# A depthwise filter's shared sum moved to ScalarE and GpSimd, and a float32 preparation made in three passes

## The chip, the cores and the metric

The kernel runs on one core of a Trainium2 chip. The metric is device time of one execution in microseconds (us), the median over the runs. The engines of the core that matter here are TensorE (PE in the profile, with PEld for its weight loads), VectorE (DVE), ScalarE (ACT), GpSimd (POOL) and SyncE (SP, which issues the transfers). SBUF is the on-chip memory, PSUM the accumulators that TensorE writes.

## What is computed

A two-layer decoder trunk on 1024 tokens of width 1024. Only the first layer's mixer (the convolution layer) and the weights of the attention into 256 memory tokens are touched; the other parts (forgetting attention, squared-ReLU MLPs, final norm) follow and are the same in both kernels.

```python
def conformer_conv(h, w_pw1, b_pw1, w_dw, b_dw, ln_g, ln_b, w_pw2, b_pw2):
    u = h @ w_pw1 + b_pw1
    a, gate = jnp.split(u, 2, axis=-1)
    u = a * jax.nn.sigmoid(gate)
    u = lax.conv_general_dilated(
        u, w_dw[:, None, :].astype(u.dtype),
        window_strides=(1,), padding=[(CONV_WIDTH - 1, 0)],
        dimension_numbers=("NWC", "WIO", "NWC"),
        feature_group_count=D_MODEL) + b_dw
    u = jax.nn.silu(layernorm(u, ln_g, ln_b))
    return u @ w_pw2 + b_pw2
...
def memory_cross_attention(h, mem_n, w_q, w_k, w_v, w_o):
    q = (h @ w_q).reshape(B, S, MEM_HEADS, MEM_HEAD_DIM)
    k = (mem_n @ w_k).reshape(B, MEM_LEN, MEM_HEADS, MEM_HEAD_DIM)
    v = (mem_n @ w_v).reshape(B, MEM_LEN, MEM_HEADS, MEM_HEAD_DIM)
    s = jnp.einsum("bshd,bmhd->bhsm", q, k).astype(jnp.float32) / math.sqrt(MEM_HEAD_DIM)
    p = jax.nn.softmax(s, axis=-1)
    o = jnp.einsum("bhsm,bmhd->bshd", p.astype(v.dtype), v).reshape(B, S, D_MODEL)
    return o @ w_o
```

The convolution has 31 taps on each of 1024 channels.

## The kernel before

**Layout.** Features lie on the 128 partitions, so a 1024x1024 array is 8 chunks of 128 features by 1024 tokens, handled in two halves of 512 tokens. The residual stream `X` is a grid of 128x512 tiles.

**Split products.** Most products run in three passes of a reduced float32 type (`F32R`): each operand is split into a high part (a cast by ScalarE) and a low part (source minus high part, by VectorE, in `low`, line 148), and `passes` and `product` (up to line 269) issue low by high, high by low and high by high into one PSUM accumulator. `product` takes a plain float32 operand as a tuple of one and then issues one matmul.

**The convolution layer** (`conv_layer`). For each chunk `m` of 8: `gated_unit` makes the first product (48 matmuls for each of the gate and the value half), ScalarE takes the sigmoid (line 368), VectorE multiplies (line 370) and writes `u` with even and odd tokens apart, two buffers of it. `weights` fetches the next chunk's weights and splits them (`wh` on ScalarE, `wl` on VectorE, two of each per chunk). Then `convolve` computes the 31 taps for the even and the odd output tokens with a shared sum: `d0` and `d1` are the differences of even and odd input tokens (lines 393 and 394), `both` is the sum over 16 pair weights times the odd tokens (one multiplication on line 396, 15 multiply-adds on line 400), and each half of the output is `both` plus 16 or 15 multiply-adds with the differences (line 408). All of this is on VectorE. The 31 multiply-adds go into two accumulators, the output tiles `X[:, m, 0]` and `X[:, m, 1]`, so two independent chains stand side by side. Line 354 adds the finished chunk to the layer norm's token sums. After the eighth chunk comes the layer norm of both halves (lines 310 to 318 and `sum_of_squares`, with the split for the next product), and then the second product `pw2` (384 matmuls of 512 columns, added to the residual on line 324).

**The memory preparation** (`memory_matrices`, a generator; for the two layers and four heads each). It folds the query weights with the keys and the value weights with the output weights, 64 weight pieces of 128x1024 (`praw`, 512 KB each) in all: four for keys and values (line 461 forward: 32 matmuls of 256 columns per head), two for `mqk` (16 matmuls of 256 columns) and two for `mvo` (8 matmuls of 512 columns). Results leave through ScalarE (`o`, lines 483 and 501) and transfers to DRAM. Everything is plain float32: nothing of it is split. `conv_layer` advances the generator by `next(prep)`: four of its 32 steps stand ahead of the first convolution, two in each chunk, and the twelve left stand between the layer norm and `pw2`.

**What sets the order.** The instructions are traced in the order of the program; a planner then fixes each engine's order ahead of time. It goes by that order as a priority and by its own estimate of when an instruction can start, so that an instruction further down is put in where an engine would otherwise stand still. `tc.high_priority` moves a few small ones ahead. On the chip, each engine then runs its list in order. PSUM's eight banks are shared out as four to the preparation, two to the products of the convolution layer, two to small work (`ps`).

Of the kernel before, what the change touches and what calls it, by code (L numbers as in the profile page):

```python
# [12 lines left out]
F32 = mybir.dt.float32  # L13
F32R = mybir.dt.float32r
# [72 lines left out]
def trunk(ctx, tc, a, out):  # L87
# [16 lines left out]
    def col(name, i):  # L104
        return par[:, COLS[name] + i : COLS[name] + i + 1]
# [38 lines left out]
    def banks(n):  # L144
        return tc.tile_pool(name="pm", bufs=n, space=PSUM, reuse_waits="tile")
# [39 lines left out]

    def add_squares(acc, ch):

        sq = nrm.tile([P, HALF], F32, name="sq", tag="t", bufs=4)
# [101 lines left out]
        dve.tensor_tensor(X[:, m, sl], t, X[:, m, sl], op=ALU.add)  # L290


    def conv_layer(pm, prep):
        with tc.tile_pool(name="conv", bufs=2) as cp:
            for sl in HALVES:
                next(prep)
                load_x(X, a["xT"], sl)
            def padded():

                u = cp.tile([P, 2, (PAD + S) // 2], F32, name="u")  # L300
                pool.memset(u[:, :, : PAD // 2], 0.0)
                return u

            pairs = tap_sums(cp)

            def layer_norm(s, acc):

                nm = nrm.tile([P, 4], F32, name="nm")
                with tc.high_priority(offset=SMALL_FIRST):
                    dve.tensor_scalar(nm, token_mean(acc), -1.0, None, op0=ALU.mult)  # L310
                nmb = spread(nm)
                C = [X[:, m, HALVES[s]] for m in range(NCH)]
                for c in C:
                    dve.tensor_tensor(c, c, nmb, op=ALU.add)
                rb = spread(inverse_rms(C, LN_EPS))
                for m, c in enumerate(C):
                    dve.tensor_tensor(c, c, rb, op=ALU.mult)
                    act.activation(c, c, AF.Silu, bias=col("ln_b", m), scale=col("ln_g", m))
                    split(*(y.rearrange("p (n s) -> p s n", s=2)[:, s, :] for y in ss[m]), c)

            def add_x(m, sl, t):
                x = nrm.tile([P, HALF], F32, name="x", tag="t", bufs=4)
                nc.sync.dma_start(x, a["xT"][:, m, sl])
                dve.scalar_tensor_tensor(
                    X[:, m, sl], t, col("pw2_b", m), x, op0=ALU.add, op1=ALU.add
                )
# [12 lines left out]
            for m in range(NCH):  # L339
                if m:  # L340
                    u = padded()
                    for sl in HALVES:
                        gated_unit(pm, cp, m, ahead, hs, u[:, :, PAD // 2 :], sl)
                if m + 1 < NCH:
                    ahead = gate_weights(m + 1)
                for _ in range(2):
                    next(prep, None)

                convolve(cp, m, u, pairs[:, m])
                for s, sl in enumerate(HALVES):  # L350
                    if m == 0:
                        act.copy(acc[s], X[:, m, sl])
                    else:
                        dve.tensor_tensor(acc[s], acc[s], X[:, m, sl], op=ALU.add)
# [28 lines left out]
        dve.tensor_tensor(sums[:, :, :n], two[:, :, :, 0], two[:, :, :, 1], op=ALU.add)  # L383
        return sums

    def convolve(cp, m, u, sums):


        n, k = S // 2, TAPS // 2
        even, odd = u[:, 0, :], u[:, 1, :]  # L390
        d0 = cp.tile([P, n + k], F32, name="d0")
        d1 = cp.tile([P, n + k - 1], F32, name="d1")
        dve.tensor_tensor(d0, even[:, : n + k], odd[:, : n + k], op=ALU.subtract)
        dve.tensor_tensor(d1, even[:, 1 : n + k], odd[:, : n + k - 1], op=ALU.subtract)
        both = cp.tile([P, n], F32, name="both")
        dve.tensor_scalar(
            both, odd[:, :n], sums[:, 0:1], col("dw_b", m), op0=ALU.mult, op1=ALU.add
        )
        for j in range(1, k + 1):
            dve.scalar_tensor_tensor(  # L400
                both, odd[:, j : j + n], sums[:, j : j + 1], both, op0=ALU.mult, op1=ALU.add
            )
        out = [X[:, m, sl] for sl in HALVES]
        for s, d, taps in ((0, d0, k + 1), (1, d1, k)):
            y = both
            for j in range(taps):
                w = col("dw_w", m * TAPS + 2 * j + s)
                dve.scalar_tensor_tensor(  # L408
                    out[s], d[:, j : j + n], w, y, op0=ALU.mult, op1=ALU.add
                )  # L410
                y = out[s]

# [20 lines left out]
    def memory_matrices(pp, pq, layer):  # L433
# [9 lines left out]
        mem = pp.tile([P, NCH, MEM], F32, name="mem", bufs=1)  # L443
        nc.sync.dma_start(mem, a["memT"])
        if layer == 0:
            r = inverse_rms([mem[:, c, :] for c in range(NCH)], RMS_EPS)
# [3 lines left out]
        for c in range(NCH):  # L450
            act.activation(mem[:, c, :], mem[:, c, :], AF.Copy, scale=col(f"src{layer}", c))
        for h in range(MEM_HEADS):
            kv = []
            for w, n in ((wk, "kt"), (wv, "vt")):
                t = bank(pq).rearrange("p (c m) -> p c m", c=2)
                for c in range(2):
                    x = get(w[2 * h + c])
                    product(t[:, c, :], [((x[:, k, :],), (mem[:, k, :],)) for k in range(NCH)])
                o = pp.tile([P, 2, MEM], F32, name=n, bufs=1)
                if w is wk:  # L460
                    if layer == h == 0:
                        dve.tensor_copy(rt, r)
                        dve.tensor_copy(rs, spread(r))
                    rb = mem_r[1].unsqueeze(1).to_broadcast([P, 2, MEM])
                    with tc.high_priority(offset=SMALL_FIRST):
                        dve.tensor_tensor(o, t, rb, op=ALU.mult)
                else:
                    act.copy(o, t)
                kv.append(o)
                yield  # L470
            kt, vt = kv
            for j in range(2):

                x = get(wq[h, j])
                for g in range(2):
                    t = bank(pq).rearrange("p (f m) -> p f m", f=2)
                    o = pp.tile([P, 4, P], F32, name="o").rearrange("p (f b) n -> p f (b n)", f=2)
                    for f in range(2):
                        product(t[:, f, :], [
                            ((x[:, 4 * c + 2 * g + f, :],), (kt[:, c, :],)) for c in range(2)  # L480
                        ])
                        gain = col(f"mem{layer}", 4 * j + 2 * g + f)
                        act.activation(o[:, f, :], t[:, f, :], AF.Copy, scale=gain)
                    nc.sync.dma_start(
                        ad[:, 4 * j + 2 * g : 4 * j + 2 * g + 2, h * MEM : (h + 1) * MEM], o
                    )
            yield
            for j in range(2):

                x = get(wo[h, j])  # L490
                for mc in range(2):
                    t = bank(pq)
                    product(t, [
                        (
                            (vt[:, c, mc * P : (mc + 1) * P],),
                            (x[:, 4 * c : 4 * c + 4, :].rearrange("p b n -> p (b n)"),),
                        )
                        for c in range(2)
                    ])
# [946 lines left out]
```

## Time and profile before

| | us |
|---|---|
| median of 3 runs | 2822.2 (2816.68 to 2823.24) |
| the profiled execution | 2825.31 |
| its span, first to last instruction | 2823.3 |
| PE busy over the span | 2740.8 (97%) |
| DVE busy | 2030.9 (72%) |
| ACT busy | 1278.3 (45%) |
| POOL busy | 703.1 (25%) |

The convolution layer and the preparation fill the first 527 us of the span. The page's 40 slices are some 70 us wide; a stage is read better from windows, which give every engine's busy time in a stretch, and from the timeline. Matmuls are pipelined, so a PE that shows as busy can still take more work per unit of time if its matmuls are cheaper; the distance between starts says what a matmul costs.

### The profile page before, as it was taken

What the parts mean: (1) busy time and instruction counts of PE and PEld (TensorE: products, weight loads), DVE (VectorE), ACT (ScalarE), POOL (GpSimd) and SP (SyncE); (2) the same over time, 40 slices, a digit from 0 to 9 for tenths busy, and PEclk for the clock granted to TensorE, in tenths of its full rate; (3) what the DMA queues carried; (4) which work ended last, traced back from release to release, by engine and by line L of the source; (5) the groups of instructions that cost most, each with busy time, mean ns of one, the idle gap of its engine ahead of it and who ended that gap; (6) DMA issues with size and microseconds to landing.
All of it is one profiled execution on the core that took longest, in us unless ns stands there. A gap on an engine that the chain in (4) does not pass through costs nothing.

```text
span 2823.3 us, 36214 instructions
## 1 busy us (share of the span) xinstructions
PE 2740.8 (97%) x12968; PEld 2261.3 (80%) x12968; DVE 2030.9 (72%) x3358; ACT 1278.3 (45%) x2293; POOL 703.1 (25%) x473
## 2 busy tenths in 40 slices
PE   8999999999999999999899999989999999989998
PEld 6777777888888877888688888878888788878886
DVE  5999984555776576777788888875546855577776
ACT  5212143433555553333466666673423655543332
POOL 0000000000065625774000000000000365525773
PEclk9999999999999999999899999999999999999999
DMA  6334364322165585652222221243213455655651
GB/s 219 120 119 135 114 206 124 101 90 70 65 230 177 178 309 187 227 199 89 69 68 70 57 65 55 69 136 98 94 64 105 149 176 190 218 208 197 227 201 61
DMA packets 165428, 390.68 MB, mean 138 GB/s; under 512 B 17264, under 2 KB 46192, under 8 KB 164992
## 3 DMA queue, kind: packets, MB, share of 16 engines
q1 hardware_dynamic: 165248, 388.37, 40.9%
q8 instruction: 102, 1.67, 0.2%
q14 instruction: 78, 0.64, 0.1%
HBM read 270.79 MB, written 113.31 MB: 136 GB/s over the span
## 4 chain that ended last, share of the span: by engine, by line
PE 74%; DVE 12%; ACT 5%; DMA 5%; issue 3%; POOL 1%; SPq 0%; DVEq 0%; POOLq 0%; ACTq 0%
PE mm L1070 34%; PE mm L269 29%; PE mm L1255 5%; DVE w L148 2%; DVE op L148 2%; DVE x L408 1%; PE mm L1341 1%; DVE x L1310 1%; DMA ua<-x 1%; ACT x L1315 1%; PE mm L1353 1%; PE mm L1354 1%; DVE both L400 1%; DVE wl L148 1%; ACT pth L151 1%
## 5 line engine op out<-in xcount | busy, mean ns | idle before, releaser
L1070 PE MATMUL mm<-op,w 128*128 128x512 f32 x5424 | 1242.4, 391 | 24.5 <-ACT m L955 8.7
L1070 PEld LDWEIGHTS mm<-op,w 128*128 128x128 f32 x5424 | 1020.5, 189 | 243.2 <-ACT m L955 9.6
L269 PE MATMUL mm<-op,wh 128*128 128x512 f32 x1056 | 330.5, 394 | 4.2 <-DVE op L148 4.2
L148 DVE TENSOR_TENSOR w<-r,w 128x512 fp32r<-128x512 f32 x264 | 262.6, 998 | 30.5 <-ACT w L653 30.5
L653 ACT CAST w<-r 128x512 fp32r<-128x512 f32 x264 | 163.3, 622 | 262.0 <-PE mm L1070 233.2
L269 PEld LDWEIGHTS mm<-op,wh 128*128 128x128 f32 x1056 | 200.2, 190 | 48.5 <-DVE op L148 6.5
L1255 PE MATMUL mm<-op,wh 128*128 128x512 f32 x736 | 231.4, 396 | 0.0
L148 DVE TENSOR_TENSOR w<-t,w 128x512 fp32r<-128x512 f32 x180 | 178.2, 1005 | 63.2 <-ACT w L653 63.1
L269 PE MATMUL mm<-op,wl 128*128 128x512 f32 x528 | 210.5, 400 | 7.1 <-DVE wl L148 6.2
L207 POOL TENSOR_TENSOR r<-v,mhalf 128x4 f32<-128x4 f32 (+1 forms) x15 | 16.8, 1117 | 741.0 <-DVE v L205 741.0
L647 POOL TENSOR_TENSOR t<-r,t 128x512 f32<-128x512 f32 x104 | 174.9, 1681 | 91.4 <-DVE w L148 54.2
L653 ACT CAST w<-t 128x512 fp32r<-128x512 f32 x180 | 112.0, 622 | 169.8 <-PE mm L1070 140.6
L151 ACT CAST wh<-raw 128x1024 fp32r<-128x1024 f32 x96 | 100.7, 1050 | 193.8 <-PE mm L269 97.5
L865 POOL TENSOR_TENSOR x<-x,x 128x512 f32<-128x512 f32 x112 | 160.2, 1455 | 112.6 <-ACT x L878 101.6
L967 DVE TENSOR_TENSOR x<-mm,x 128x512 f32<-128x512 f32 x160 | 109.5, 684 | 91.1 <-PE mm L1070 73.7
L1255 PEld LDWEIGHTS mm<-op,wh 128*128 128x128 f32 x736 | 139.2, 189 | 26.7
L269 PE MATMUL mm<-op,xsh 128*128 128x512 f32 x512 | 158.0, 393 | 0.0
L1255 PE MATMUL mm<-op,wl 128*128 128x512 f32 x368 | 155.0, 421 | 1.9 <-ACT q L1275 1.9
L151 ACT CAST pth<-mm 128x512 fp32r<-128x512 f32 (+1 forms) x224 | 105.9, 495 | 108.5 <-PE mm L556 80.8
L408 DVE SCALAR_TENSOR_TENSOR x<-d,par,x 128x512 f32<-128x512 f32 x232 | 154.5, 746 | 0.0
L647 POOL TENSOR_TENSOR t<-r,r 128x512 f32<-128x512 f32 x52 | 80.2, 1542 | 295.1 <-DMA r<-in_ff_w 191.0
L1315 ACT ACTIVATE x<-x,nb 128x128 f32<-128x128 f32 (+7 forms) x128 | 99.5, 778 | 109.3 <-DVE nb L1313 100.0
(188 smaller groups left out, 4689.6 us busy)
## 6 DMA issues: line engine op xcount, KB each, us to landing
r<-in_ff_w SPq DMA_DIRECT2D x128, 512.0 KB, 4.0
op<-ua SPq DMA_DIRECT2D x80, 512.0 KB, 6.8
us<-x SPq DMA_DIRECT2D x128, 256.0 KB, 2.9
op<-us SPq DMA_DIRECT2D x64, 512.0 KB, 5.6
raw<-mvo SPq DMA_DIRECT2D x32, 512.0 KB, 3.4
ua<-ul SPq DMA_DIRECT2D x64, 256.0 KB, 2.2
ua<-uh SPq DMA_DIRECT2D x60, 256.0 KB, 2.3
raw<-in_pw SPq DMA_DIRECT2D x24, 512.0 KB, 4.7
```

Of the source, the lines that this page charges most:

```text
L148: dve.tensor_tensor(lo, src, hi.bitcast(F32), op=ALU.subtract)
L151: act.copy(hi, src)
L269: pe.matmul(out_ps, x, y, start=i == 0, stop=i == len(terms) - 1)
L400: dve.scalar_tensor_tensor(both, odd[:, j : j + n], sums[:, j : j + 1], both, op0=ALU.mult, op1=ALU.add)
L408: dve.scalar_tensor_tensor(out[s], d[:, j : j + n], w, y, op0=ALU.mult, op1=ALU.add)
L647: (dve if g in (2, 3, UP, UP + 1) else pool).tensor_tensor(t, raws[g, x], raws[g, y], op=ALU.subtract)
L653: act.copy(highs[n][0], raws[steps[n][:2]])
L865: eng.tensor_tensor(u[g, x], y1, y2, op=op_)
L967: dve.tensor_tensor(v, sums[key], v, op=ALU.add)
L1070: pe.matmul(sums[key], y, z, start=first and i == 0, stop=n == last_of[key] and i == len(terms) - 1, skip_group_check=True,)
L1255: pe.matmul(t, x, y, start=n == 0, stop=n == len(terms) - 1)
L1315: act.activation(x[:, :n], x[:, :n], AF.Exp, bias=nb, accum_out=rs)
```

## The change

Four things are done together.

- `both` is made by ScalarE and GpSimd: 16 activations with a per-partition scale make the terms (tiles `tap` of the shared tag `t`, four buffers), and GpSimd adds 15 of them to the first.
- The 31 multiply-adds on VectorE go through one PSUM bank `acc` (from a pool of one bank, `pc`), even half first and then odd half; only the last tap of a half writes `X`. `d0` and `d1` have one buffer instead of two. The preparation has three PSUM banks instead of four.
- The preparation's products are made of split operands, three matmuls in place of one. Each weight piece is fetched as two halves of 256 KB (three buffers), each cast by ScalarE and its low part formed by VectorE (128 of each over the stage). The memory tokens are split as well (16 small multiply-subtracts on VectorE), and so are the keys and values.
- The memory tokens arrive in four transfers of two chunks through the same buffers, with the squares taken chunk by chunk.

```diff
     def convolve(cp, pc, m, u, sums):
...
-        dve.tensor_scalar(
-            both, odd[:, :n], sums[:, 0:1], col("dw_b", m), op0=ALU.mult, op1=ALU.add
-        )
-        for j in range(1, k + 1):
-            dve.scalar_tensor_tensor(
-                both, odd[:, j : j + n], sums[:, j : j + 1], both, op0=ALU.mult, op1=ALU.add
-            )
-        out = [X[:, m, sl] for sl in HALVES]
+        both = cp.tile([P, n], F32, name="both")
+        act.activation(both, odd[:, :n], AF.Identity, scale=sums[:, 0:1], bias=col("dw_b", m))
+        for j in range(1, k + 1):
+            t = nrm.tile([P, HALF], F32, name="tap", tag="t", bufs=4)
+            act.activation(t, odd[:, j : j + n], AF.Copy, scale=sums[:, j : j + 1])
+            pool.tensor_tensor(both, both, t, op=ALU.add)
+        d0 = cp.tile([P, n + k], F32, name="d0", bufs=1)
+        d1 = cp.tile([P, n + k - 1], F32, name="d1", bufs=1)
...
+        acc = bank(pc)
         for s, d, taps in ((0, d0, k + 1), (1, d1, k)):
             y = both
             for j in range(taps):
+                o = X[:, m, HALVES[s]] if j == taps - 1 else acc
                 w = col("dw_w", m * TAPS + 2 * j + s)
-                dve.scalar_tensor_tensor(
-                    out[s], d[:, j : j + n], w, y, op0=ALU.mult, op1=ALU.add
-                )
-                y = out[s]
+                dve.scalar_tensor_tensor(o, d[:, j : j + n], w, y, op0=ALU.mult, op1=ALU.add)
+                y = acc
...
+        def half(src):
+            raw = pp.tile([P, NCH // 2, P], F32, name="praw", bufs=3)
+            nc.sync.dma_start(raw.rearrange("p k n -> p (k n)"), src.rearrange("p k n -> p (k n)"))
+            return raw
+
         def get(src):
-            raw = pp.tile([P, NCH, P], F32, name="praw", bufs=3)
-            nc.sync.dma_start(raw, src)
-            return raw
+            halves = []
+            for i in range(2):
+                raw = half(src[:, 4 * i : 4 * i + 4, :])
+                hi, lo = (pp.tile([P, NCH // 2, P], F32R, name=f"p{x}", bufs=3) for x in "hl")
+                act.copy(hi, raw)
+                dve.tensor_tensor(lo, raw, hi.bitcast(F32), op=ALU.subtract)
+                halves.append((hi, lo))
+            return halves
...
-                    product(t[:, c, :], [((x[:, k, :],), (mem[:, k, :],)) for k in range(NCH)])
-                o = pp.tile([P, 2, MEM], F32, name=n, bufs=1)
+                    product(t[:, c, :], [
+                        ([y[:, k % 4, :] for y in x[k // 4]], (memh[:, k, :], meml[:, k, :])) for k in range(NCH)
+                    ])
+                hi, lo = (pp.tile([P, 2, MEM], F32R, name=n + y, bufs=1) for y in "hl")
...
-    with prep_pools(4) as pools, banks(2) as pm:
-        conv_layer(pm, chain(*(memory_matrices(*pools, l) for l in range(2))))
+    with prep_pools(3) as pools, banks(2) as pm, banks(1) as pc:
+        conv_layer(pm, pc, chain(*(memory_matrices(*pools, l) for l in range(2))))
```

The two other products of the preparation take split operands in the same way.

More of the change, by code (lines that the diff above doesn't have):

```diff
@@ L436, in memory_matrices @@
         ad, vd = mats[layer]
+        def half(src):
+            raw = pp.tile([P, NCH // 2, P], F32, name="praw", bufs=3)
+            nc.sync.dma_start(raw.rearrange("p k n -> p (k n)"), src.rearrange("p k n -> p (k n)"))
+            return raw
         def get(src):
-            raw = pp.tile([P, NCH, P], F32, name="praw", bufs=3)
-            nc.sync.dma_start(raw, src)
-            return raw
-        mem = pp.tile([P, NCH, MEM], F32, name="mem", bufs=1)
-        nc.sync.dma_start(mem, a["memT"])
+            halves = []
[6 more added lines that the diff above has]
+            return halves
+        memh, meml = (pp.tile([P, NCH, MEM], F32R, name=f"mem{x}", bufs=1) for x in "hl")
+        sums = None
+        for c in range(NCH):
+            if c % 2 == 0:
+                two = half(a["memT"][:, c : c + 2, :]).rearrange("p (c k) n -> p c (k n)", c=2)
+            ch, g = two[:, c % 2, :], col(f"src{layer}", c)
+            if layer == 0:
+                sums = add_squares(sums, ch)
+            act.activation(memh[:, c, :], ch, AF.Copy, scale=g)
+            dve.scalar_tensor_tensor(
+                meml[:, c, :], ch, g, memh[:, c, :].bitcast(F32), op0=ALU.mult, op1=ALU.subtract
+            )
         if layer == 0:
-            r = inverse_rms([mem[:, c, :] for c in range(NCH)], RMS_EPS)
+            with tc.high_priority(offset=SMALL_FIRST):
+                r = rms_of_sums(sums, RMS_EPS)
             rt = const.tile([P, MEM // P], F32, name="mem_r")
@@ L479, in memory_matrices @@
                         product(t[:, f, :], [
-                            ((x[:, 4 * c + 2 * g + f, :],), (kt[:, c, :],)) for c in range(2)
+                            ([y[:, 2 * g + f, :] for y in x[c]], [y[:, c, :] for y in kt]) for c in range(2)
                         ])
```

24 lines of the change are left out of this document (11 added, 13 removed).

## The prediction

> **What bounds the kernel now.** The change touches only the first 527 us, so I start with the windows of that stretch (columns: the stretch, its length, then busy time and instruction count of PE, PEld, DVE, ACT and POOL, granted clock, transfers).
>
> ```profile
> core 0: us, PE busy (x) PEld busy (x) DVE busy (x) ACT busy (x) POOL busy (x), PEclk, DMA share, GB/s
> 50.00:77.00 27.00, 27.00 (x105) 19.70 (x105) 13.32 (x20) 12.13 (x17) 0.00 (x0) 0.99 0.34 98
> 77.00:389.00 312.00, 307.35 (x1299) 243.55 (x1298) 306.57 (x441) 63.69 (x106) 0.75 (x6) 1.00 0.43 136
> 389.00:431.00 42.00, 41.22 (x198) 31.96 (x198) 30.66 (x52) 27.37 (x50) 2.01 (x2) 1.00 0.60 185
> 431.00:527.00 96.00, 96.00 (x414) 76.95 (x412) 41.30 (x55) 33.10 (x50) 0.00 (x0) 1.00 0.33 101
> ```
>
> From 77 to 389 (the eight convolutions) VectorE is busy 306.57 of 312 us and TensorE 307.35: both are full, while ScalarE and GpSimd are almost free. From 389 to 431 the layer norm passes between engines and TensorE fills in with preparation; from 431 `pw2` has TensorE full and VectorE under half busy. So up to 389 **two** engines bound the stage. Work taken from one of them alone gives nothing there. What the change does to VectorE before `pw2` decides.
>
> One chunk of VectorE's list, in order of time (start, us, engine, line, operation, count):
>
> ```profile
> 151.48 1.41 DVE L370 SCALAR_TENSOR_TENSOR u<-mm,par,sg 128x512 f32<-128x512 f32 x2
> 152.81 2.35 DVE L148 TENSOR_TENSOR wl<-raw,wh 128x1024 fp32r<-128x1024 f32 x2
> 155.08 0.70 DVE L393 TENSOR_TENSOR d<-u 128x527 f32<-128x527 f32 x1
> ...
> 158.04 0.54 DVE L396 TENSOR_SCALAR both<-u,sums,par 128x512 f32<-128x512 f32 x1
> 158.61 11.78 DVE L400 SCALAR_TENSOR_TENSOR both<-u,sums,both 128x512 f32<-128x512 f32 x15
> 170.43 1.42 DVE L408 SCALAR_TENSOR_TENSOR x<-d,par,both 128x512 f32<-128x512 f32 x2
> 171.76 19.30 DVE L408 SCALAR_TENSOR_TENSOR x<-d,par,x 128x512 f32<-128x512 f32 x29
> 190.97 1.29 DVE L354 TENSOR_TENSOR acc<-acc,x 128x512 f32<-128x512 f32 x2
> 192.18 1.41 DVE L370 SCALAR_TENSOR_TENSOR u<-mm,par,sg 128x512 f32<-128x512 f32 x2
> ```
>
> `both` takes 170.43 - 158.04 = 12.4 us of the chunk, the 31 taps 190.97 - 170.43 = 20.5. The two chains have the same kind of instruction but another pace: 15 in 11.78 us is 0.785 each where each needs the one before; 29 in 19.30 is 0.666 where two chains alternate. The dependent one shows 0.12 us of stall per tap.
>
> **TensorE: 46 us less, and not where it counts.** Rows that give the distance between starts:
>
> ```profile
> 99.77 0.39 PE L269 MATMUL mm<-op,wl 128*128 128x512 f32 x1
> 100.44 0.39 PE L269 MATMUL mm<-op,wl 128*128 128x512 f32 x1
> 124.25 3.60 PE L269 MATMUL mm<-praw,vt 128*128 128x512 f32 x8
> 1611.83 0.28 PE L1354 MATMUL mm<-pth,vs 128*128 128x256 f32 x1
> 1611.94 0.28 PE L1353 MATMUL mm<-ptl,vs 128*128 128x256 f32 x1
> L269 PE MATMUL mm<-mem,praw 128*128 128x256 f32 x512 | 116.7, 386 | 9.1 <-ACT mem L451 8.7 <-DMA praw<-in_mem_wk 0.5
> L269 PE MATMUL mm<-kt,praw 128*128 128x256 f32 x256 | 61.2, 385 | 6.0 <-ACT o L483 4.5 <-DMA praw<-in_mem_wq 1.4
> ```
>
> Three split matmuls of 512 columns start 0.67 us apart in all (0.224 each); one of 256 columns takes 0.11. A plain float32 matmul is two records: 8 records of 512 columns take 3.60 us, so one matmul 0.86, and one of 256 columns about 0.43 (the 768 records stand for 384 matmuls). Preparation before: 384 x 0.43 + 64 x 0.86 = 220 us. After: 384 x 3 x 0.113 + 64 x 3 x 0.226 = 174 us. TensorE saves 46 us of the stage; 83% of the preparation's records lie before 389:
>
> ```profile
> 0.00:77.00 77.00, 34.54 (x118) 0.96 0.61 207
> 77.00:350.00 273.00, 117.05 (x469) 1.00 0.38 121
> 350.00:389.00 39.00, 38.01 (x159) 1.00 0.76 243
> ```
>
> (118 + 469 + 159 of 896.) So TensorE gets slack before 389 and stands waiting for VectorE.
>
> **VectorE from 77 to the last tap, term by term.**
>
> 1. `both` goes: 8 x 12.4 = **-99 us**.
> 2. The taps become one chain through one PSUM bank, since the odd half must wait for the even half's `acc`. Nothing in the trace writes PSUM from VectorE. Bounds: no stall (0.666) to 0.87 (the stall doubled); I take the dependent row, 0.785: 8 x (31 x 0.785 - 20.5) = **+30 us**, range 0 to +51.
> 3. Low parts. 128 over the stage; 83% are 106, of which some 16 fit the idle half of VectorE before 77. A 128x512 instruction with two inputs holds the engine 0.61 us (line 354's row above: two in 1.29, of which the second's own 0.69 falls away); put into a tap's stall it adds 0.61 - 0.12 = 0.49. 90 x 0.49 = 44, with 13 low parts of keys and values 6, and the second layer's memory tokens 3: **+53 us**. That the planner puts such work into a dependent chain shows in a later chunk, where `u` stands inside `both`:
>
> ```profile
> 275.99 8.63 DVE L400 SCALAR_TENSOR_TENSOR both<-u,sums,both 128x512 f32<-128x512 f32 x11
> 284.53 0.75 DVE L370 SCALAR_TENSOR_TENSOR u<-mm,par,sg 128x512 f32<-128x512 f32 x1
> ```
>
> 4. **GpSimd beside VectorE.** Now it is idle here. Later, in the MLP, it adds 128x512 tiles while VectorE forms low parts:
>
> ```profile
> 850.00:950.00 100.00, 100.00 (x443) 82.84 (x442) 60.67 (x76) 56.26 (x95) 60.12 (x42) 1.00 0.50 174
> L148 DVE TENSOR_TENSOR w<-r,w 128x512 fp32r<-128x512 f32 x84 | 86.7, 1033 | 11.1 <-ACT w L653 11.1
> L148 DVE TENSOR_TENSOR op<-op 128x1024 fp32r<-128x1024 f32 x30 | 45.0, 1500 | 0.0
> L967 DVE TENSOR_TENSOR x<-mm,x 128x512 f32<-128x512 f32 x49 | 33.5, 684 | 28.9 <-PE mm L1070 21.5 <-POOL x L924 7.4
> L647 POOL TENSOR_TENSOR t<-r,t 128x512 f32<-128x512 f32 x36 | 61.9, 1720 | 28.7 <-DMA ua<-ul 14.2 <-DVE w L148 13.1
> L865 POOL TENSOR_TENSOR x<-x,x 128x512 f32<-128x512 f32 x35 | 49.3, 1433 | 0.7
> L148 DVE TENSOR_TENSOR op<-h,op 128x512 fp32r<-128x512 f32 x16 | 10.9, 689 | 0.5 <-ACT op L222 0.4
> L148 DVE TENSOR_TENSOR wl<-raw,wh 128x1024 fp32r<-128x1024 f32 x26 | 31.1, 1220 | 12.5 <-ACT wh L151 12.1 <-DMA x<-in_xT 0.4
> ```
>
> With GpSimd busy 60.12 of 100 us a low part with both inputs in SBUF takes 1033 ns against 689 in the convolution stage (1500 against 1220 for the long one), while the addition with one input in PSUM (`x<-mm,x`) stays at 684. So the taps through `acc` should escape this and the rest not. GpSimd's 120 additions at 1.5 us are 180 us of the 345 from 77 to the last tap, or 0.52: 0.34 x 0.52/0.60 = 0.29 us for each low part it meets. The instructions are 90 low parts, 16 `wl`, 16 `d`, 16 additions of line 354 and 16 first taps, 154, of which the last chunk's eighth has no addition beside it: 135 x 0.29 = **+39 us**, range 0 (additions and low parts miss each other) to +52 (154 x 0.34).
>    The Trainium skill ("SBUF — State Buffer", section "Who interferes with whom") has VectorE and GpSimd exclude each other: the second to come waits until the first is done. By that rule a low part waits half an addition, 0.75 us, in 0.52 of the cases, and the term is 135 x 0.39 = +53. The trace agrees that PSUM inputs escape; it shows less than the full wait.
>    The Trainium skill ("VectorE: DVE Perf Modes", section on the TRN2 errata) also gives 120 fixed cycles from PSUM against 58 from SBUF, which would be an estimated 65 ns on each of 248 taps, or +16 us. The trace speaks against it for reads, 684 from PSUM and 689 from SBUF, so the sum leaves it out.
> 5. **The first chunk's wait.** Its 15 additions at 1.4 to 1.5 us are some 22 us after `u`, and no earlier chunk covers them. VectorE has about 11 us to do meanwhile (`d`, `wl`, `u` of the next chunk, low parts): **+11 us**, range 0 to +15. For later chunks the sum runs under the taps before, if `u` is written early (third rival).
>
> Sum: -99 + 30 + 53 + 39 + 11 = **+34 us**, last tap at 423 instead of 389.
>
> **ScalarE** gets 16 terms a chunk and 128 casts. Prices, with and without a scale:
>
> ```profile
> L182 ACT ACTIVATE t<-x 128x512 f32<-128x512 f32 x42 | 24.7, 625 | 9.3 <-DVE acc L183 4.9 <-DVE x L324 4.3
> L318 ACT ACTIVATE x<-x,par 128x512 f32<-128x512 f32 x16 | 12.1, 806 | 0.0
> ```
>
> Some 16 x 0.7 = 11 us and 13 casts x 0.62 = 8 us on top of 63.69/8 = 8 us a chunk: 27 of about 41. Hidden under VectorE and GpSimd; without that cover it would cost the same 27.
>
> **After the last tap.** 22 low parts are left, 13 us; the layer norm leaves VectorE 42 - 30.66 = 11 us: +3. With TensorE ahead, `pw2` finds no preparation left before it: 384 x 0.226 = 87 us instead of 96, less 4 until the second half's norm is through: -5. The four smaller token transfers and the early casts move the start by a few us either way; I take nothing.
>
> **Total: +34 + 3 - 5 = +32 us** on the profiled execution's 2825.3 (span 2823.3 and 2.0 around it), which lies 3.1 above the median of 2822.2. On the median: **2854 us**.
>
> **The rivals.**
>
> - *Faster.* TensorE's saving shows because VectorE is relieved after all: writing PSUM hides the stall (term 2 at 0, though a low part then costs 0.61, +12) and low parts fall clear of the additions (term 4 at 0). For it: low parts and additions wait on different things, and PSUM inputs do escape. Against it: dependent steps stall in the one row there is. 32 - 39 - 30 + 12 = -25: **2797 us**. It decides once terms 2 and 4 together come to less than some 37 us. Chance 0.23.
> - *No change.* Only term 4 vanishes: 32 - 39 = -7, **2815 us**. Chance 0.14.
> - *Much slower: the sum comes late in every chunk.* At 192.18 `u` is written after the taps and not before. If that order stays, each chunk waits for 22 us of additions with some 9 us of work beside it: 7 x 13 = 91 more, **2945 us**. ScalarE's waits on its own stores make it worse:
>
> ```profile
> ACT o L501 <- DMA mqk<-o: 25.0, 9, 5.1
> ACT o L501 <- DMA mvo<-o: 20.3, 9, 4.2
> ACT o L483 <- DMA mqk<-o: 14.9, 10, 3.6
> ```
>
>   60 us in which the terms would queue behind it. Against it: `u` has two buffers, TensorE gets slack, and a single chain lets the planner put `u` inside. Chance 0.13.
>
> **The numbers.** Forecast (2854, its own range 2836 to 2870) 0.50; the rivals as given. A measurement of this kernel can tell about 0.3%, 8.5 us, from no change. Faster 0.23, within 0.14 and a little of the forecast's lower end, 0.16, slower 0.61. Range: the full bounds of terms 2 and 4 above are +21 and +13, to 2888; the faster rival takes the other end; the late sum is left out. **2795 to 2890.**
>
> **What would show it.** Taps at 0.78 us in one chain, or at 0.67; low parts at 0.95 us and not 0.69 while GpSimd adds; VectorE still full to about 420 with TensorE showing gaps; `pw2` in 87 to 90 us. Wrong would be: VectorE idle at the start of each chunk's taps with GpSimd named (third rival), TensorE still full before the layer norm (first), or a last tap before 390.

## The result, and the profile after

| | before | after |
|---|---|---|
| median, us | 2822.3 (2816.68 to 2823.24, 4 runs) | 2948.0 (2947.17 to 2949.47, 4 runs) |
| profiled execution, us | 2825.31 | 2947.17 |
| its span, us | 2823.3 | 2945.1 |
| last tap, us | 387.8 | 448.3 |
| preparation matmuls issued after the last tap | 154 of 896 | 408 of 1344 |
| end of `pw2` (last line 324), us | 526.3 | 642.9 |

The ratio is 1.045, 95% interval 1.0432 to 1.0468. The rest of the span, from the end of `pw2` on, took 2302.2 us after 2297.0, so the loss lies in the convolution layer: 60.5 us up to the last tap and 56.1 us between it and the end of `pw2`.

The view to begin with is the windows from 77 us to the end of `pw2`, first of the kernel before, then of the changed one (columns as in the prediction: length, then PE, PEld, DVE, ACT, POOL, granted clock).

```profile
77.00:526.30 449.30, 443.87 (x1906) 352.03 (x1905) 377.93 (x547) 123.51 (x203) 2.76 (x8) 1.00 0.42 133
```

```profile
77.00:642.90 565.90, 450.99 (x2324) 375.43 (x2323) 413.19 (x556) 277.84 (x457) 174.61 (x128) 0.91 0.36 111
```

TensorE was idle for 449.3 - 443.9 = 5.4 us before and for 565.9 - 451.0 = 114.9 us after. That difference, 109.5 us, is nearly all of the loss of 116.6. And TensorE's busy time has not fallen, though the cheaper matmuls were to save 46 us. Part of the reason is its clock, which falls while it waits (0.91 on average), so that what it does next takes longer: busy time multiplied by the missing share of the clock, in windows of 2 us, comes to an estimated 20 us, against nothing before. What else keeps the busy time up isn't shown. Slices of the changed kernel show where TensorE idles:

```profile
300.00:350.00 50.00, 44.46 (x234) 36.49 (x232) 48.18 (x65) 27.62 (x45) 25.68 (x20) 0.99 0.36 111
350.00:400.00 50.00, 35.64 (x166) 29.29 (x167) 44.17 (x52) 27.99 (x48) 30.09 (x21) 0.84 0.41 125
400.00:450.00 50.00, 10.37 (x68) 9.59 (x66) 47.53 (x72) 7.99 (x13) 0.00 (x0) 0.61 0.13 38
450.00:500.00 50.00, 27.37 (x125) 23.38 (x126) 34.50 (x58) 30.52 (x50) 2.02 (x2) 0.64 0.03 11
500.00:550.00 50.00, 43.97 (x292) 38.29 (x293) 22.43 (x33) 29.14 (x51) 0.00 (x0) 1.00 0.79 236
```

Between 400 and 500 TensorE works 38 of 100 us, and the last column (GB/s) says that hardly anything is being fetched either: the preparation has stopped at about 410 us, though 30% of its matmuls are still to come. Most of them are done from 500 on, in front of most of `pw2`. The timeline of SyncE's queue and of ScalarE and VectorE tells why:

```profile
408.95 2.84 SPq L439 DMA_DIRECT2D praw<-in_mem_wo  x2
496.15 2.44 SPq L508 DMA_DIRECT2D mqk<-o  x2
498.69 1.19 SPq L439 DMA_DIRECT2D praw<-in_mem_wo  x2
408.99 0.62 ACT L448 CAST ph<-praw 128x512 fp32r<-128x512 f32 x1 [0.31 <-DVE pl L449]
436.39 0.63 ACT L179 ACTIVATE acc<-x 128x512 f32<-128x512 f32 x1 [26.79 <-DVE x L314]
476.37 0.63 ACT L182 ACTIVATE t<-x 128x512 f32<-128x512 f32 x1 [0.17 <-DVE acc L183]
477.16 0.69 DVE L489 TENSOR_TENSOR kt<-mm,mem_rs 128x512 f32<-128x512 f32 x1
```

The scaled keys `kt` of the next head stand in the shared tag `t`, whose four buffers go round in program order. The layer norm's squares (line 182) use the same tag and were traced earlier, so `kt` comes at 477.16, behind the last of the squares (476.37), and behind it stand the head's products and the stores and fetches of SyncE.

Up to the last tap the wait groups from 77 to 448 us, on VectorE, are (us in total, times, longest):

```profile
DVE mm L409 <- POOL both L398: 17.0, 2, 10.4
DVE vtl L148 <- ACT vth L151: 12.9, 3, 6.5
DVE pl L449 <- ACT ph L448: 9.6, 7, 4.3
DVE wl L148 <- ACT wh L151: 3.9, 1, 3.9
```

VectorE waits twice for the shared sum (17.0 us), and longer for casts of ScalarE (26.4 us). The taps in a chain, in VectorE's timeline:

```profile
418.10 11.05 DVE L409 SCALAR_TENSOR_TENSOR mm<-d,par,mm 128x512 f32<-128x512 f32 x14
```

And the instructions that meet, by form from 77 to 450 us (busy us, mean ns of one):

```profile
L398 POOL TENSOR_TENSOR both<-both,tap 128x512 f32<-128x512 f32 x120 | 172.0, 1433 | 127.4 <-ACT tap L397 119.1
L409 DVE SCALAR_TENSOR_TENSOR mm<-d,par,mm 128x512 f32<-128x512 f32 x216 | 162.0, 750 | 3.3
L449 DVE TENSOR_TENSOR pl<-praw,ph 128x512 fp32r<-128x512 f32 x76 | 70.1, 926 | 9.7 <-ACT ph L448 9.6
L409 DVE SCALAR_TENSOR_TENSOR mm<-d,par,both 128x512 f32<-128x512 f32 x16 | 15.4, 965 | 17.2 <-POOL both L398 17.0
L354 DVE TENSOR_TENSOR acc<-acc,x 128x512 f32<-128x512 f32 x14 | 14.3, 1019 | 0.1
```

### The profile page after: what moved, and what is told of

The parts are those of the page before. It is cut to its first block, busy times and chain, and to the rows that moved or that the text cites. A ratio compares the mean times of both kernels' runs of the same rounds, so it can differ in the third digit from the quotient of the medians.

```text
span 2945.1 us, 37886 instructions
## 1 busy us (share of the span) xinstructions
PE 2737.4 (93%) x13416; PEld 2281.6 (77%) x13416; DVE 2077.2 (71%) x3390; ACT 1437.2 (49%) x2557; POOL 872.9 (30%) x593
## 4 chain that ended last, share of the span: by engine, by line
PE 66%; DVE 16%; ACT 6%; DMA 5%; issue 4%; POOL 3%; SPq 0%; POOLq 0%; DVEq 0%; ACTq 0%
PE mm L1094 35%; PE mm L269 20%; PE mm L1279 5%; DVE mm L409 4%; POOL both L398 2%; DVE op L148 2%; DVE w L148 1%; DVE pl L449 1%; PE mm L1365 1%; DVE x L1334 1%; ACT x L1339 1%; DVE wl L148 1%; PE mm L1377 1%; PE mm L1378 1%; PE mm L158 1%
## 5 line engine op out<-in xcount | busy, mean ns | idle before, releaser
L269 PE MATMUL mm<-op,wh 128*128 128x512 f32 x1056 | 339.4, 401 | 4.6 <-DVE op L148 4.5
L1279 PE MATMUL mm<-op,wh 128*128 128x512 f32 x736 | 230.6, 394 | 0.0
L398 POOL TENSOR_TENSOR both<-both,tap 128x512 f32<-128x512 f32 x120 | 172.0, 1433 | 127.4 <-ACT tap L397 119.1
L409 DVE SCALAR_TENSOR_TENSOR mm<-d,par,mm 128x512 f32<-128x512 f32 x216 | 162.0, 750 | 3.3
```

Source lines behind the costliest of these rows:

```text
L269: pe.matmul(out_ps, x, y, start=i == 0, stop=i == len(terms) - 1)
L398: pool.tensor_tensor(both, both, t, op=ALU.add)
L409: dve.scalar_tensor_tensor(o, d[:, j : j + n], w, y, op0=ALU.mult, op1=ALU.add)
L1279: pe.matmul(t, x, y, start=n == 0, stop=n == len(terms) - 1)
```

## The experiments

All ratios are to the kernel before, run again beside each (medians of 2817.9 to 2822.5 us), with 95% intervals. "TensorE idle" is the length of the window from 77 us to the end of `pw2` less PE's busy time in it.

| kernel | median us | ratio | last tap | end of `pw2` | TensorE busy / idle |
|---|---|---|---|---|---|
| before | 2822.3 | | 387.8 | 526.3 | 443.9 / 5.4 |
| after | 2948.0 | 1.0450 [1.0432, 1.0468] | 448.3 | 642.9 | 451.0 / 114.9 |
| e1_own_keys | 2906.7 | 1.0305 [1.0284, 1.0327] | 452.9 | 603.9 | 446.8 / 80.1 |
| e2_conv_only | 2910.5 | 1.0320 [1.0297, 1.0342] | 451.2 | 610.0 | 461.2 / 71.8 |
| e3_prep_only | 2960.1 | 1.0500 [1.0478, 1.0521] | 450.7 | 658.6 | 452.1 / 129.5 |
| e3k_prep_only_own_keys | 2936.0 | 1.0410 [1.0387, 1.0433] | 444.1 | 630.3 | 438.7 / 114.6 |
| e5_conv_ahead | 2875.7 | 1.0193 [1.0170, 1.0216] | 421.0 | 579.1 | 458.1 / 44.0 |
| e9_conv_deep_taps | 2907.7 | 1.0309 [1.0292, 1.0326] | 452.8 | 611.4 | 463.2 / 71.2 |
| e8_ahead_deep_taps | 2826.3 | 1.0011 [0.9998, 1.0024] | 371.9 | 531.0 | 443.6 / 10.4 |
| e6_own_keys_ahead | 2937.5 | 1.0410 [1.0387, 1.0434] | 492.1 | 635.1 | 446.8 / 111.3 |
| e11_all_ahead_deep_taps | 2909.1 | 1.0320 [1.0292, 1.0348] | 463.5 | 606.2 | 447.3 / 81.9 |
| e13_all_lows_first | 2914.2 | 1.0330 [1.0311, 1.0349] | 476.8 | 607.6 | 444.6 / 86.0 |
| e7_layer1_split_ahead | 2918.1 | 1.0341 [1.0314, 1.0368] | 444.4 | 615.4 | 452.9 / 85.5 |
| e10_layer1_split_only | 2897.1 | 1.0271 [1.0255, 1.0286] | 406.9 | 593.6 | 440.8 / 75.8 |
| e12_layer1_ahead_deep_taps | 2882.6 | 1.0218 [1.0195, 1.0242] | 406.7 | 578.7 | 441.5 / 60.2 |
| e14_layer1_lows_first | 2872.6 | 1.0182 [1.0164, 1.0199] | 422.3 | 569.1 | 442.3 / 49.8 |
| e15_layer1_lows_gpsimd | 2880.3 | 1.0217 [1.0193, 1.0242] | 418.4 | 584.7 | 454.2 / 53.5 |
| e16_layer1_lows_both | 2871.3 | 1.0201 [1.0165, 1.0236] | 421.1 | 568.6 | 445.7 / 45.9 |

The last column is the thread: in all of them TensorE is busy for 439 to 463 us, and what it idles makes most of the difference.

### The shared slots

```diff
-                        o = nrm.tile([P, HALF], F32, name="kt", tag="t", bufs=4)
-                        o = o.rearrange("p (c m) -> p c m", c=2)
+                        o = pp.tile([P, 2, MEM], F32, name="kt", bufs=1)
```

> The changed kernel with one edit: the scaled keys go into a tile of their own in the preparation's pool instead of a tile of the tag t that the taps and the layer norm's squares rotate through. Theory (shared slots): the keys of the last three heads stand behind the layer norm's squares in that tag, so the preparation stops at 411 us and TensorE idles through the layer norm; with the edit the preparation goes on, pw2 starts some 60 to 75 us earlier, and the median falls from 2948 to 2873 to 2890 us. Rival (the feeding: three half pieces in flight and casts late in ScalarE's list starve the preparation): the order of the slots changes little, 2935 to 2955 us.

Measured: 41 us less than the changed kernel, where 58 to 75 were expected. The time from the last tap to the end of `pw2` fell from 194.6 to 151.0 us (138.5 before the change), while the last tap came 4.6 us later. So the shared slots are shown to be most of the loss behind the last tap, and none of that ahead of it.

### Each part alone

e2 has the new filter with the plain preparation, e3 the split preparation with VectorE's filter of before, and e3k the same with the keys in their own tile (and `d0`, `d1` in one buffer each, for the room).

> The kernel before with the new filter alone (terms on ScalarE, additions on GpSimd, taps through one PSUM bank, one bank less for the preparation); the preparation stays plain float32. Theory: VectorE's list shrinks by some 40 us before the layer norm, TensorE stays full and sets the end, so 2805 to 2825 us. Rival (the sum comes late in each chunk whatever the preparation does): VectorE waits 5 us or more per chunk on GpSimd, 2850 to 2900 us.

> The changed kernel with the filter of before (everything on VectorE, taps into X, four banks for the preparation); the split preparation and its keys in the tag t stay. Theory (shared slots): VectorE has the low parts on top of both, last tap near 440, and the preparation's last heads are held behind the layer norm's squares as in the changed kernel: 2920 to 2960 us. Rival (the hold-up needs the taps' buffers or GpSimd): the preparation runs on through the layer norm, 2860 to 2890 us.

> As the kernel with the split preparation alone, with the keys in a tile of their own and one buffer each for d0 and d1 (to make room). Theory (shared slots): 55 to 75 us less than the same without the edit, 2860 to 2890 us. Rival (the feeding): within 15 us of it.

Each part alone loses about as much as both together: 90 us for the filter, 140 for the preparation, 116 with its own keys. The own keys are worth 24 us there, not the 55 to 75 expected. That the filter costs nothing by itself, the theory for e2, fell. Its trace is that of the third rival, in the waits from 77 to 450 us and in VectorE's timeline:

```profile
DVE mm L409 <- POOL both L398: 116.0, 8, 17.4
ACT tap L397 <- POOL both L398: 43.9, 68, 1.0
```

```profile
163.84 0.75 DVE L370 SCALAR_TENSOR_TENSOR u<-mm,par,sg 128x512 f32<-128x512 f32 x1
...
173.80 1.77 DVE L402 TENSOR_TENSOR d<-u 128x526 f32<-128x526 f32 x1
187.62 0.76 DVE L409 SCALAR_TENSOR_TENSOR mm<-d,par,both 128x512 f32<-128x512 f32 x1 [12.06 <-POOL both L398]
```

The next chunk's `u` is complete at 164.6, late in the taps of the chunk before; the sum takes 23 us from there; VectorE has 11 us to do meanwhile and stands 12.06. In e2 this comes in every chunk (8 waits). In the changed kernel it came only twice. What differs is the split preparation; that its low parts stretch a chunk's taps and so cover the sum is the likely reason, but no run tested that alone.

### What the filter needs: a lead, and buffers

e5 is e2 with one chunk's lead: product, `u` and sum of chunk m + 1 are traced ahead of the taps of chunk m, and the first tap stands behind that `u` in VectorE's list. e9 is e2 with ten buffers for the terms. e8 has both.

```diff
             for m in range(NCH):
-                if m:
+                now = u, both
+                if m + 1 < NCH:
                     u = padded()
                     for sl in HALVES:
-                        gated_unit(pm, cp, m, ahead, hs, u[:, :, PAD // 2 :], sl)
...
+                        gated_unit(pm, cp, m + 1, ahead, hs, u[:, :, PAD // 2 :], sl)
+                    written = nc.cur_bb.bb.instructions[-1].name
+                    both = shared_sum(cp, m + 1, u, pairs[:, m + 1])
...
-                convolve(cp, pc, m, u, pairs[:, m])
+                convolve(cp, pc, m, *now, written)
```

```diff
-            t = nrm.tile([P, HALF], F32, name="tap", tag="t", bufs=4)
+            t = cp.tile([P, HALF], F32, name="tap", bufs=10)
```

> The kernel with the new filter alone (plain preparation), with one chunk's lead written into the program: the product of chunk m+1 and its shared sum are traced before the taps of chunk m, and the first tap of m stands behind the last multiplication of u for m+1 in VectorE's list. Theory (late sum as a loop: u of the next chunk stands some 20 taps down in this chunk's list, and its 23 us of additions start only then, so a chunk takes 20 taps plus the sum, 44 to 47 us instead of 39): VectorE's waits on the sum, 116 us in the filter alone, shrink to about 15 (the first chunk), and the time falls from 2910 to 2815 to 2840 us. Rival (GpSimd or ScalarE cannot keep the pace, or the port between VectorE and GpSimd costs it): it stays above 2880 us.

> Plain preparation, the new filter with one chunk's lead as in the earlier run with the lead, and ten buffers of their own for the scaled taps instead of the four that they shared. Theory (ScalarE's list is paced by GpSimd through the four buffers, and the sigmoids and copies behind the terms come late): ScalarE writes its terms at 0.72 us each without waiting, the waits of VectorE for sg (14.7 us in one place) go, the idle time of VectorE before the last tap falls from 89 us to under 50, the last tap comes at 375 to 395 instead of 421, time 2790 to 2840. Rival (GpSimd's 15 additions of 1.43 us, 21.5 us a chunk, or the order of the lists themselves set the pace): last tap still after 410, time over 2860.

> Plain preparation, the new filter without the lead, ten buffers for the scaled taps. Theory (without the lead the sum starts only when the next chunk's u is written, late in the chunk before, and then takes GpSimd's 21.5 us whatever ScalarE does): VectorE still waits for the sum in each chunk, over 90 us in all, time 2890 to 2915, as with four buffers (2910). Rival (the pacing of ScalarE alone makes the loss): under 2870.

From 2910 the lead alone took 35 us, the buffers alone 3, both together 84, and the filter's loss was gone. e8 and e9 came out as their theories had it; e5 lies between its theory and its rival. With the lead VectorE no longer waits for the sum (116.0 us in e2, 116.1 in e9), but in e5 TensorE waits 27.5 us for ScalarE's copies of preparation products (line 494), which in e8 are 0.6. ScalarE's timeline shows what the buffers do, in e5:

```profile
78.90 3.16 ACT L398 ACTIVATE tap<-u,sums 128x512 f32<-128x512 f32 x5
82.76 0.72 ACT L398 ACTIVATE tap<-u,sums 128x512 f32<-128x512 f32 x1 [0.69 <-POOL both L399]
...
94.94 0.72 ACT L398 ACTIVATE tap<-u,sums 128x512 f32<-128x512 f32 x1 [0.62 <-POOL both L399]
95.57 0.67 ACT L373 ACTIVATE sg<-mm,par 128x512 f32<-128x512 f32 x1
```

and in e8:

```profile
73.39 9.30 ACT L398 ACTIVATE tap<-u,sums 128x512 f32<-128x512 f32 x15
82.59 0.67 ACT L373 ACTIVATE sg<-mm,par 128x512 f32<-128x512 f32 x1
```

With four buffers ScalarE writes a term only when GpSimd has added an earlier one, at GpSimd's pace, and the sigmoid that stands behind starts 16.7 us after the first scaled term (78.90 to 95.57) instead of 9.2. With ten it does not wait there.

That e8 is no faster than before is as telling: its VectorE was busy 250.1 us from 77 to the last tap where it was 305.4, and the last tap came 15.9 us earlier. But TensorE stayed full, in the window from 77 us to the end of `pw2`:

```profile
77.00:531.00 454.00, 443.58 (x1884) 349.14 (x1882) 315.33 (x416) 199.15 (x326) 162.55 (x127) 0.99 0.40 131
```

### The split preparation with these remedies

e6 is e1 with the lead, e11 the same with deep buffers: the terms go through the tiles of `X` whose chunks aren't written yet, then through tag `t`. e7, e12 and e10 split the second layer's preparation only, with the keys in a tile of their own: e7 with the lead, e12 with lead and deep buffers, e10 with VectorE's filter of before.

```diff
-            t = nrm.tile([P, HALF], F32, name="tap", tag="t", bufs=4)
+            i = (j - 1) % (2 * (NCH - m) + 4)
+            if i < 2 * (NCH - m):
+                t = X[:, NCH - 1 - i // 2, HALVES[i % 2]]
+            else:
+                t = nrm.tile([P, HALF], F32, name="tap", tag="t", bufs=4)
```

> The changed kernel with the keys in a tile of their own and the same lead of one chunk. Theory: the shared slots and the late sum are the two things beyond VectorE's own work; with both gone the last tap comes at some 400 to 420 us and pw2 ends near 540 to 560, 2840 to 2870 us, which is what the sum on record foresaw without them. Rival (low parts wait on casts behind the taps in ScalarE's list): little changes against the own keys alone, 2890 to 2910 us.

> The whole change with the three remedies: scaled keys in a tile of their own, the shared sum one chunk ahead, and deep buffers for the scaled taps (they go through the rows of X of chunks not yet written, 4 to 20 buffers, which need no memory). Theory (late sum, ScalarE paced through four buffers and the shared slots are all of the loss but the low parts' own time): the 45 us that VectorE idles ahead of the last tap when the preparation is plain take in half of the 107 low parts of 0.75 us ahead of it, last tap at 400 to 420, time 2810 to 2850, against 2937 without the deep buffers. Rival (the casts come late on ScalarE for another reason, so that preparation products stay behind the last tap): over 2880.

> As the last one, with the preparation split for the second layer only (its low parts fall where VectorE has room: the last chunks, the layer norm and pw2) and plain for the first. Theory: TensorE saves some 23 us where it sets the end, VectorE has 64 low parts instead of 128 and is relieved of both: 2800 to 2825 us. Rival (the low parts of the second layer still hold the preparation behind the layer norm): 2840 to 2880 us.

> The same with the split form for the second layer's preparation only. Theory: 64 low parts, about 23 to 40 of them ahead of the last tap, fit into VectorE's idle time, and TensorE, busy in nearly all of the stretch before the second product, saves half of 46 us: last tap at 372 to 390, time 2790 to 2825. Rival (the split form costs on the way what TensorE saves, as with VectorE's filter, where one layer cost 75 us): over 2850.

> The filter of before on VectorE alone, the scaled keys in a tile of their own, and the preparation in split form for the second layer only. Theory (each low part put on VectorE ahead of the last tap delays it, and each preparation product left behind the last tap delays the second product of the convolution): half of what the split of both layers costs (2936 less 2820, 116 us), so 2860 to 2895, last tap near 415. Rival (the second layer's preparation lies late, where it has cover under the layer norm): under 2840.

The lead on four buffers made things worse (e6, 31 us over e1). Of VectorE's waits from 77 to 492 us in e6, the first two are casts:

```profile
DVE pl L461 <- ACT ph L460: 59.3, 20, 7.8
DVE wl L148 <- ACT wh L151: 21.5, 3, 15.0
```

The deep buffers gave 28 us (e6 to e11) and 36 us (e7 to e12), and VectorE's waits for `ph` up to the last tap fell from 59.3 us in e6 to 20.4 in e11. But all five theories were too hopeful (that of e10 by 2 us): beside the mended filter the split form still costs 83 us for both layers (e11 against e8) and 56 for one (e12), and with VectorE's filter one layer costs 75 (e10). In e10 TensorE waits 36.3 us for low parts, and 18.9 in one place for the token sums of the layer norm, which need the last tap. Its timeline and VectorE's show both:

```profile
383.36 0.55 PE L269 MATMUL mm<-memh,pl 128*128 128x256 f32 x1 [2.50 <-DVE pl L457]
...
408.14 1.86 PE L158 MATMUL mm<-mean_col,acc 128*128 128x1 f32 x8 [18.93 <-DVE acc L354]
```

```profile
385.66 0.68 DVE L457 TENSOR_TENSOR pl<-praw,ph 128x512 fp32r<-128x512 f32 x1
386.26 1.40 DVE L408 SCALAR_TENSOR_TENSOR x<-d,par,both 128x512 f32<-128x512 f32 x2
387.59 19.29 DVE L408 SCALAR_TENSOR_TENSOR x<-d,par,x 128x512 f32<-128x512 f32 x29
406.81 1.28 DVE L354 TENSOR_TENSOR acc<-acc,x 128x512 f32<-128x512 f32 x2
408.01 0.68 DVE L457 TENSOR_TENSOR pl<-praw,ph 128x512 fp32r<-128x512 f32 x1
```

Between two low parts stand all 31 taps. TensorE was idle for the whole of 390 to 400 us: the next product in its list is the layer norm's, and the next one of the preparation needs the low part behind the same taps.

### The low parts' place, and their engine

e13 (both layers, on e11) and e14 (second layer, on e12) give casts and low parts priority; e15 and e16 are e14 with all or every second low part on GpSimd.

```diff
-                act.copy(hi, raw)
-                dve.tensor_tensor(lo, raw, hi.bitcast(F32), op=ALU.subtract)
+                with tc.high_priority(offset=SMALL_FIRST):
+                    act.copy(hi, raw)
+                    dve.tensor_tensor(lo, raw, hi.bitcast(F32), op=ALU.subtract)
```

> The whole change with the three remedies, and the casts and low parts of the preparation's weights written as early in ScalarE's and VectorE's lists as their data allow (a priority ahead of the taps and of the shared sum's terms). Theory (TensorE, busy in 477 of 483 us before, starves because a low part stands behind a run of taps on VectorE, and its cast behind the sum's terms on ScalarE): TensorE's waits for low parts, 63.8 us with the casts and low parts in program order, fall under 25, time 2850 to 2880 against 2909. Rival (the low parts' own time on a full VectorE, and the three buffers of each part, make the wait; the place in the list only moves it to the taps): 2895 to 2925.

> The same for the version that splits the second layer's preparation only. Theory: TensorE's waits for low parts, 49 us in program order, fall under 20, time 2830 to 2860 against 2883. Rival (the place in the list only moves the wait): 2870 to 2890.

> The second layer split, remedies as before, and GpSimd instead of VectorE forms the 64 low parts of the weights (it idles once the sums are done, at about 345 us). Theory (what is left of the loss is VectorE's own time for low parts ahead of the last tap): the last tap comes at 375 to 395 as in the plain version with the lead and deep buffers (372), against 422, time 2815 to 2850. Rival (a low part on GpSimd takes 1.43 us where TensorE uses one up in about 672 x 0.12 / 64 = 1.26 us, so TensorE starves on GpSimd's pace): 2855 to 2890.

> The same with every second low part on VectorE and the others on GpSimd. Theory: last tap at 390 to 405, TensorE's waits for low parts under 15 us, time 2820 to 2855. Rival (either engine's place in its list still holds TensorE): 2860 to 2880.

In e13 TensorE's waits for low parts fell from 63.8 to 26.3 us and the preparation was done at 468.9, ahead of the last tap; but that came 13 us later, the layer norm behind it had no preparation left for TensorE to do, and the time is the same, as the rival had it. e14 gained 10 us and lies in its rival's range: TensorE's waits for low parts fell from 49.0 to 10.6 us, but 15.4 for `vtl` and 14.0 for ScalarE's copies (line 560) took their place.

e15 and e16 came out at their rivals' times as well. Taking low parts off VectorE did not bring the last tap forward: 418 and 421 after 422. The windows up to the last tap, of e14 and then of e15, say why:

```profile
77.00:422.30 345.30, 311.70 (x1499) 253.91 (x1498) 293.30 (x385) 178.33 (x297) 165.79 (x126) 0.98 0.39 128
```

```profile
77.00:418.40 341.40, 311.41 (x1442) 254.17 (x1441) 266.49 (x339) 170.66 (x283) 215.51 (x166) 0.96 0.37 119
```

In e14 VectorE was busy for 43.2 us more than in e8 (250.1); its 47 low parts take 38.6, and the last tap came 50.4 us later. So the low parts' own time, my theory for e15 and e16, does make most of e14's delay. But in e15 VectorE has 26.8 us less to do and idles for 22.9 us more (74.9 after 52.0), while TensorE waits 19.9 us for the low parts of GpSimd, as the rival had it. VectorE's timeline in e15 shows where it idles:

```profile
336.71 1.06 DVE L419 SCALAR_TENSOR_TENSOR mm<-d,par,both 128x512 f32<-128x512 f32 x1
345.00 0.69 DVE L148 TENSOR_TENSOR vtl<-mm,vth 128x512 fp32r<-128x512 f32 x1 [7.22 <-ACT vth L151]
...
360.23 3.13 DVE L419 SCALAR_TENSOR_TENSOR mm<-d,par,mm 128x512 f32<-128x512 f32 x4
375.25 0.69 DVE L520 TENSOR_TENSOR kt<-mm,mem_rs 128x512 f32<-128x512 f32 x1 [11.90 <-PE mm L269]
```

The keys' and values' steps wait on VectorE for preparation products, and taps that could run stand behind them, while TensorE waits for low parts. This ring of in-order lists is read from the trace of e15 alone: in e16, with half of the low parts on GpSimd, VectorE waits 0.5 us for `kt`, but 19.9 for casts (`ph`). No run took `kt` and `vtl` out of the taps' way, and none gave the split weight halves and their parts more than three buffers, so whether the split preparation can be had without the loss stays open.

## Why the prediction was wrong

The direction was right; the time lies 94 us above the forecast and outside the range. By its steps, the profiled executions' difference of 121.9 us (5.2 of it behind `pw2`) against the 32 forecast:

- **Both engines are full, work taken from one gives nothing.** Right, and shown by e8: 55 us less work on VectorE, the same time.
- **VectorE's own work, terms 1 to 4 (+23).** Measured +13.7 (319.1 us busy from 77 to the last tap, after 305.4). Term 2 was right: 14 taps of one chain through PSUM took 11.05 us, 0.789 each (0.785 taken). (Its upper bound, 0.87, isn't the doubled stall that it is called: 0.666 + 2 x 0.12 is 0.90, and would give some +60 instead of +51.) Term 3 was near as a sum: with VectorE's filter of before (e3k) the split added 45.7 us of busy time up to the last tap (351.1 after 305.4), where 53 was taken, but with 69 low parts ahead of that tap and not 90, for which its own prices give some 41. Term 4 was right in kind: taps through PSUM stay at 750 ns, while low parts took 926 against 689 (76 x 0.24 = 18 us), line 354 1019 and the first taps 965 (8 us more), `d` 1179 and 1039 (6.5 more), and `wl` as before: some 33 us against 39. By the rule of the Trainium skill ("SBUF — State Buffer", section "Who interferes with whom") it would have been 53; the low parts took 0.24 us more each, where that rule has 0.39.
- **Term 5 and "ScalarE ... Hidden" (+11).** The first wait for the sum was 10.4 us, as worked out. But VectorE's idle time up to the last tap grew from 5.4 to 52.2 us, and the sum makes only 17.0 of it: 26.4 more are casts of ScalarE that come late (`vth`, `ph`, `wh`). I compared ScalarE's busy time with the chunk's length and found room; its list is in order and, as e5 and e8 show, goes at GpSimd's pace through four buffers. That this pace makes the casts late is seen in e6 and e11 (waits for `ph` of 59.3 us with four buffers, 20.4 with more); for the changed kernel itself it is argued. This step failed: 47 us measured where 11 were taken.
- **"With TensorE ahead, `pw2` finds no preparation left before it" (-2 with the low parts left).** Measured +56.1, the largest miss. TensorE was not ahead: 30% of the preparation lay behind the last tap, 17% before the change. Some 44 us of it is the shared tag (e1): the change puts `kt` into it, and I did not follow that tag to the layer norm.
- **"TensorE saves 46 us, and not where it counts."** The saving isn't seen in its busy time (451 after 444), an estimated 20 us of it because its clock falls while it waits; and its gaps, which the sum puts at nothing, are 109.5 of the 116.6 us lost by the end of `pw2`.
- **The third rival** gave 2945, within 3 us of the time, by another mechanism: seven late sums of 13 us. The changed kernel shows two, 17.0 us in all. That mechanism is real where the filter stands alone (116.0 us in e2); here the number agrees by chance.

## What to carry to other kernels

Where two engines are full, work out the idle time that a change makes on each of them, not only the work that it takes away: here the time followed TensorE's gaps closely in every version. Work that was handed to slower engines needed a lead of a whole step and buffers for the difference in pace, both at once (35 and 3 us alone, 84 together). And a rotating buffer shared by two stages ties them in program order; before adding a user to it, look for who took a slot just ahead.

## What the runs showed of the hardware

The granted clock follows the gaps quickly. The changed kernel's windows of 10 us (third column from the end) have its clock at half while it idles:

```profile
400.00:410.00 10.00, 6.43 (x52) 6.02 (x50) 9.69 (x16) 3.58 (x6) 0.00 (x0) 1.00 0.46 141
410.00:420.00 10.00, 0.00 (x0) 0.00 (x0) 9.68 (x15) 0.00 (x0) 0.00 (x0) 0.53 0.17 52
420.00:430.00 10.00, 0.00 (x0) 0.00 (x0) 9.54 (x14) 0.00 (x0) 0.00 (x0) 0.50 0.00 0
```

and in e10, after 2.50 us of waiting, split matmuls start 0.21 us apart instead of 0.12:

```profile
380.22 0.28 PE L269 MATMUL mm<-memh,ph 128*128 128x256 f32 x1
380.34 0.28 PE L269 MATMUL mm<-memh,pl 128*128 128x256 f32 x1
...
383.92 0.41 PE L269 MATMUL mm<-memh,ph 128*128 128x256 f32 x1
384.14 0.41 PE L269 MATMUL mm<-memh,pl 128*128 128x256 f32 x1
```

The Trainium skill ("TensorE: Matmul & The Clock Gate", Part 1) has the clock halve once TensorE has idled for a window of some 3.4 us; the 0.50 agrees. The length does not: in e10 the granted clock was 0.94 from 382 to 383 us and 0.50 from 383 to 386, some 2 us after TensorE's last matmul had ended. So a cheaper matmul that had to wait for its operands gave back less here than its price says.
